# Pauses ahead of two mixer steps, a first norm fed by a spread row, and a norm in one operation, in a fp32 encoder trunk on one core

## The chip, the cores and the metric

The kernel runs on one core of a Trainium2 chip. Its time is device microseconds (us) per execution; the median of three runs before is 1455.33 us (1454.59 to 1459.27).

## The reference

Two layers work on 256 tokens of width 1024, in float32. Each is a half-step feed-forward block, a mixer of three branches (GLA, S5, FoX), a cross attention to 256 memory tokens, and a second feed-forward block. Every block has a norm before and behind it:

```
def rms_norm(x, g):
    y = x * rsqrt(mean(x * x) + EPS)
    return y * g
for l in range(DEPTH):
    x = x + 0.5 * rms_norm(swiglu(rms_norm(x, ffn1_pre_g), w_gu, w_down), ffn1_post_g)
    p = rms_norm(x, mix_pre_g) @ w_in         # GLA's q, k, v, gates; S5's input u; FoX's q, k, v; branch gates
    x = x + rms_norm((sum_b sigmoid(gate_b) * up_b(mixer_b)) @ w_mix_out, mix_post_g)
    x = x + rms_norm(cross_attn(rms_norm(x, xa_pre_g), rms_norm(mem)), xa_post_g)
    x = x + 0.5 * rms_norm(swiglu(rms_norm(x, ffn2_pre_g), w_gu, w_down), ffn2_post_g)
```

In GLA, `g = cumsum(log_a)` sets decays: keys are multiplied by `exp(g_last - g)` for the chunk states, and by `exp(-g)` and `exp(g)` for the products inside a chunk. S5 is a complex scan whose output `y` goes through a gelu and a 256x256 gate product.

## The kernel before

Every matrix is kept as a high and a low part (`wh`, `wl`, `xth`, `xtl`: `split`, L234), and each product is three TensorE passes (`mm3`, L248). Weights stream from HBM in pieces of 128x1024 (512 KB): SyncE issues the transfer into one of five `wf` buffers, ScalarE casts it to `wh`, VectorE subtracts for `wl`; seven `wh`/`wl` pairs form a ring, so about five pieces stand ready ahead of TensorE. One half of a `proj_cols` takes one piece and 24 products of 256 columns.

Each engine runs its instructions in the order in which the program text gives them. Side work (GLA, S5, FoX, the S5 set-up) is written as generators; `run_tasks` is called after each half of a projection (a tick) and advances each by one step; `yield n` puts off the next step by n ticks. `finish` runs a generator to its end at once, whatever pauses are left. So a `yield` sets where a step's instructions stand in every engine's queue, and not a time.

GLA (`gla`, L798): `gla_gates` forms z, g and the three exponentials; then VectorE multiplies keys (L815 to L817: `dg` is the key with its decay), TensorE transposes `dg` (L821), ScalarE copies it out (L823); VectorE then forms `qb` (L827, L829), which the products at L840 read; the o products are L866 and L869; the last transposes are L889. S5 (`s5`, L896): L910 and L922 are its first products, the scan is L926, L945 the output products, L954 the gelu's last step; then `yd` is written to DRAM (L958), read back in another layout as `yv` (L961), and `yv` is the operand of L967. In the FoX projections L1003 copies TensorE's result out, and L1007 writes rows of `fq` that a transfer of a one-hot table (L993) fills first.

A block's end is `boundary` (L446). Token tile 0's last products are done first, and its norm runs on ScalarE, VectorE and GpSimd beside tile 1's products: `post2` (L412) updates x, `pre1` squares x on ScalarE (L381), multiplies x by the gain on VectorE (L419, L422), adds the sums (L387), GpSimd raises to -1/2 (L388), and `scale` (L427) multiplies by that factor; TensorE then transposes (L433).

The start (`run`, `first`): twelve warm products of zeros; transfers of tile 0 of x, of the gain (one row spread to 128 partitions by the transfer, 512 KB), of the identity, of two weight pieces, of tile 1, of more weights. `first` norms tile 0, transposes it and multiplies it by the first four pieces (`go(0)`, L336) while tile 1 is normed; then transposes tile 1 and runs `go(1)`. Two of the first `wl` are made by GpSimd.

Of the kernel before, what the change touches and what calls it, by code (L numbers as in the profile page):

```python
# [8 lines left out]
F32 = mybir.dt.float32  # L9
# [4 lines left out]
ALU = mybir.AluOpType  # L14
# [6 lines left out]
EPS = 1e-6  # L21
# [9 lines left out]
WB = 7  # L31
WF = 5
HALF = 1024
WARM = 12
TAIL = 5

C_ID, C_FM, C_P2, C_HM, C_END = 0, 128, 512, 520, 524
# [17 lines left out]
class Trunk:  # L55
# [23 lines left out]
    def make_plan(self, depth):  # L79
        a = self.a  # L80
        self.plan, self.parts = [], []

        def add(ap, n=2048):
            for c in range(0, n, HALF):
                self.plan.append(ap[:, c:min(c + HALF, n)])

        def ffn(l, i):
            gu, dn = a[f"ffn{i}_gu"], a[f"ffn{i}_dn"]
            q = 0
            for j in range(NFT):  # L90
                add(gu[l, j])
                if j >= 4 and j % 2 == 0:
                    n = min(q + 2, NFT - TAIL)
                    for k in range(q, n):
                        add(dn[l, k], D)
                    q = n
            for k in range(q, NFT):
                add(dn[l, k], D)
            self.parts.append(len(self.plan))

        for l in range(depth):
            ffn(l, 1)
            for q in range(2):
                add(a["w_gvr"][l, q])
            add(a["w_small"][l], 512)
            for q in (0, 1, 2, 4):
                add(a["w_cols"][l, q])
            for q in range(2):
                add(a["w_fv"][l, q])

            def gate(b, c):
                add(a["w_cols"][l, 6 + 4 * b + c])

            def up(b, c):
                if b == 2:
                    add(a["w_fup"][l, c], 1024)
                else:
                    add(a["w_up"][l, b, c], 512)

            for c in (0, 1):  # L120
                gate(0, c)
            for q in (3, 5):
                add(a["w_cols"][l, q])
            for b, c in ((0, 0), (0, 2), (2, 0), (2, 2)):
                if (b, c) != (0, 0):
                    gate(b, c)
# [16 lines left out]
        self.pool_every = 0  # L143


    def house(self, homes):
# [13 lines left out]
            self.raw[self.n_dma] = (wf, n)  # L160
            self.n_dma += 1

    def split_next(self, eng=None):
# [12 lines left out]
        if eng is None and self.pool_every and i % self.pool_every == 0:  # L176
            eng = self.nc.gpsimd
        self.split(h[:, 0:n], lo[:, 0:n], wf[:, 0:n], eng)
        self.ready[i] = (h, lo)
        self.n_split += 1  # L180
        self.fetch(i + 1 + WF)

    def ahead(self, lag=1):
        while self.room(lag):
# [46 lines left out]
            self.ahead()  # L231


    def split(self, h, lo, src, eng=None, vector=False):  # L234
# [5 lines left out]
        (eng or self.nc.vector).tensor_tensor(full(lo), src, h.bitcast(F32), op=ALU.subtract)  # L240

    def split_ps(self, h, lo, ps):
        h, src = full(h), full(ps)
# [168 lines left out]
            self.nc.vector.scalar_tensor_tensor(xx, o, r, xx, op0=ALU.mult, op1=ALU.add)  # L412

    def pre1(self, src, g):
        V = self.nc.vector
        hn = self.work()
        o, i, gg = halves(hn), halves(src), halves(g)
        ss = [self.sumsq(i[0], 0)]
        V.tensor_tensor(o[0], i[0], gg[0], op=ALU.mult)  # L419
        ss.append(self.sumsq(i[1], 1))  # L420
        r = self.rstd(ss, EPS)
        V.tensor_tensor(o[1], i[1], gg[1], op=ALU.mult)  # L422
        return hn, r

    def scale(self, hn, r):
        for h in halves(hn):
            self.nc.vector.tensor_scalar(h, h, r, None, op0=ALU.mult)  # L427

    def turn(self, hn, q):
        ps = self.bank()  # L430
# [15 lines left out]
    def boundary(self, banks, tail, half, width=None, fill=None):  # L446
        nc = self.nc
        go_tail, last = tail
        gpost, gpre = self.gp, self.gn
        self.ahead(0)  # L450
        go_tail(0)
        square, times, second = self.post1(banks[0], gpost, half)
        square(0)
        times(0)
        y0 = second()
        xt = self.xt()
        st = {}

        def turn(t, q):
            self.pre3(t, q, self.turn(st[t], q), xt)  # L460

        def early():
            self.post2(0, *y0)
            h0, r0 = self.pre1(self.x[:, 0], gpre)
            st["p1"] = self.post1(banks[1], gpost, half)
            st["p1"][0](0)
            self.scale(h0, r0)
            st["p1"][1](0)
            st[0] = h0
            turn(0, 0)  # L470

        self.free(last)
        go_tail(1, (2 * last - 1, early))
        p = self.turn(st[0], 1)
        y1 = st["p1"][2]()
        self.pre3(0, 1, p, xt)

        def late():
            self.post2(1, *y1)
            h1, r1 = self.pre1(self.x[:, 1], gpre)  # L480
            self.scale(h1, r1)
            st[1] = h1
# [12 lines left out]
        self.free(4)  # L495
        self.ahead()
        return xt, ps

    def store(self, banks, tail):
        nc, out = self.nc, self.a["out"]  # L500
        for t in range(2):
# [5 lines left out]
            for n, (o, xx) in enumerate(zip(halves(y), halves(self.x[:, t]))):  # L507
                nc.vector.scalar_tensor_tensor(xx, o, r, xx, op0=ALU.mult, op1=ALU.add)
                nc.sync.dma_start(out[t * 128:(t + 1) * 128, n * 512:(n + 1) * 512], xx)

    def first(self, g, width):
        V = self.nc.vector
        xt = self.xt()

        def norm(t):
            hn = self.work()
            r = self.rstd([self.sumsq(x, n) for n, x in enumerate(halves(self.x[:, t]))], EPS)
            for o, x, gg in zip(halves(hn), halves(self.x[:, t]), halves(g)):
                V.scalar_tensor_tensor(o, x, r, gg, op0=ALU.mult, op1=ALU.mult)
            return hn  # L520

        h = norm(0)
        p0 = self.turn(h, 0)
        p1 = self.turn(h, 1)
        self.split_next(self.nc.gpsimd)
        self.pre3(0, 0, p0, xt, True)
        self.pre3(0, 1, p1, xt)
        self.split_next()
        h = norm(1)
        self.split_next(self.nc.gpsimd)  # L530
        out, go = self.head(width)
        go(0, xt)
        self.turned(1, h, xt)
        go(1, xt)
        self.free(4)
        self.ahead()
        return xt, out
# [263 lines left out]
    def gla(self, l, psm, vg, sgg, com, pool):  # L801
# [14 lines left out]
        V.tensor_tensor(kie, ks, ieg, op=ALU.mult)  # L816
        V.tensor_tensor(keg, ks, eg, op=ALU.mult)  # L817
        S.copy(ae, eg[:, 63:255:64])
        pkt = self.pbank(1)
        for t in range(2):  # L820
            T.transpose(pkt[:, t * 128:(t + 1) * 128], kd[:, t * 128:(t + 1) * 128], ident)  # L821
# [75 lines left out]
    def s5(self, l, com):  # L897
# [5 lines left out]
        def tt(o, x, y, op):  # L903
            V.tensor_tensor(o, x, y, op=op)

        yield 3
        vr, vi = self.bank(), self.bank()
        for i, v in enumerate((vr, vi)):
            for j in range(8):
# [419 lines left out]
    def run(self, depth=L):  # L1329
# [4 lines left out]
        nc.vector.memset(zero, 0.0)  # L1334
        zero = zero.rearrange("p a b -> p (a b)").bitcast(BF16)
        warm = self.bank()
        for i in range(WARM):
# [179 lines left out]
```

## Time and profile before

| | |
|---|---|
| median of 3 runs | 1455.33 us |
| the profiled execution | 1458.61 us, span 1456.8 us, mean granted TensorE clock 0.990 |
| TensorE products busy | 1425.2 us (98%) |
| VectorE, ScalarE, GpSimd busy | 936.4 us (64%), 715.2 us (49%), 68.8 us (5%) |
| transfers | 257.52 MB, 177 GB/s on average |

TensorE's share counts a product that runs at half clock as busy too, so what it loses stands in two places: idle time ahead of an instruction (with what ended it), and stretches in which the granted clock (PEclk) is 0.50, that is 1.2 instead of 2.4 GHz.

### The profile page before, as it was taken

What the parts mean: (1) busy time and instruction counts of PE and PEld (TensorE: products, weight loads), DVE (VectorE), ACT (ScalarE), POOL (GpSimd) and SP (SyncE); (2) the same over time, 40 slices, a digit from 0 to 9 for tenths busy, and PEclk for the clock granted to TensorE, in tenths of its full rate; (3) what the DMA queues carried; (4) which work ended last, traced back from release to release, by engine and by line L of the source; (5) the groups of instructions that cost most, each with busy time, mean ns of one, the idle gap of its engine ahead of it and who ended that gap; (6) DMA issues with size and microseconds to landing.
All of it is one profiled execution on the core that took longest, in us unless ns stands there. A gap on an engine that the chain in (4) does not pass through costs nothing.

```text
span 1456.8 us, 24663 instructions
## 1 busy us (share of the span) xinstructions
PE 1425.2 (98%) x9972; PEld 1314.7 (90%) x9972; DVE 936.4 (64%) x1408; ACT 715.2 (49%) x1129; POOL 68.8 (5%) x60
## 2 busy tenths in 40 slices
PE   8999998999999999999999999989999999999998
PEld 7999988889979989999999999888899898899997
DVE  6787566766587667555577775666556866665553
ACT  5444446355455545444454455454544655454442
POOL 1000000000210000000001000000012100000000
PEclk9999999999999999999999999999999999999999
DMA  7664637245566436655646556362565474375551
GB/s 282 217 195 144 214 121 215 93 130 180 201 213 212 149 131 206 210 186 181 203 147 215 175 194 191 126 191 91 159 222 162 162 237 160 103 248 184 188 189 44
DMA packets 76034, 257.52 MB, mean 177 GB/s; under 512 B 8688, under 2 KB 11792, under 8 KB 75920
## 3 DMA queue, kind: packets, MB, share of 16 engines
q1 hardware_dynamic: 75920, 255.95, 54.0%
q8 instruction: 78, 1.28, 0.3%
q14 instruction: 36, 0.29, 0.1%
HBM read 253.82 MB, written 2.10 MB: 176 GB/s over the span
## 4 chain that ended last, share of the span: by engine, by line
PE 86%; DVE 5%; ACT 4%; issue 2%; DMA 2%; POOL 1%; SPq 0%; DVEq 0%; POOLq 0%; ACTq 0%
PE mm L250 57%; PE pa L250 21%; PE mm L336 3%; ACT wh L239 1%; DVE wl L240 1%; PE mm L433 1%; DMA wf<-in_xa_k 1%; ACT junk L381 1%; DVE acc L1213 1%; POOL rr L388 1%; PE mm L1053 1%; PE mm L727 1%; PE pa L945 0%; PE mm L910 0%; DVE xtl L1210 0%
## 5 line engine op out<-in xcount | busy, mean ns | idle before, releaser
L240 DVE TENSOR_TENSOR wl<-wf,wh 128x1024 fp32r<-128x1024 f32 (+1 forms) x436 | 520.2, 1206 | 264.6 <-ACT wh L239 263.6
L250 PE MATMUL mm<-xth,wh 128*128 128x256 f32 (+1 forms) x2000 | 570.1, 285 | 0.0
L250 PE MATMUL mm<-xth,wl 128*128 128x256 f32 (+1 forms) x2000 | 567.5, 284 | 0.0
L250 PE MATMUL mm<-xtl,wh 128*128 128x256 f32 (+1 forms) x2000 | 566.7, 283 | 0.0
L239 ACT CAST wh<-wf 128x1024 fp32r<-128x1024 f32 (+1 forms) x442 | 446.0, 1029 | 154.3 <-PE mm L250 63.4
L250 PEld LDWEIGHTS mm<-xth,wh 128*128 128x128 f32 (+1 forms) x2000 | 379.0, 190 | 4.0 <-issue 2.1
L250 PEld LDWEIGHTS mm<-xtl,wh 128*128 128x128 f32 (+1 forms) x2000 | 377.2, 189 | 1.8
L250 PEld LDWEIGHTS mm<-xth,wl 128*128 128x128 f32 (+1 forms) x2000 | 377.9, 189 | 0.0
L250 PE MATMUL pa<-wh,hl 128*128 128x512 f32 x320 | 125.3, 392 | 0.0
L250 PE MATMUL pa<-wl,hh 128*128 128x512 f32 x320 | 125.2, 391 | 0.0
L250 PE MATMUL pa<-wh,hh 128*128 128x512 f32 x320 | 124.8, 390 | 0.0
L558 ACT ACTIVATE sil<-mm 128x256 f32<-128x256 f32 (+1 forms) x96 | 35.1, 366 | 118.0 <-PE mm L250 109.8
L239 ACT CAST hh<-h 128x256 fp32r<-128x256 f32 x80 | 32.5, 406 | 100.5 <-DVE h L560 100.5
L560 DVE TENSOR_TENSOR h<-sil,mm 128x256 f32<-128x256 f32 (+1 forms) x96 | 38.0, 396 | 60.7 <-ACT sil L558 60.7
L388 POOL TENSOR_TENSOR rr<-rv,mhalf 128x1 f32<-128x1 f32 x36 | 27.9, 775 | 954.8 <-DVE rv L387 954.8
L250 PEld LDWEIGHTS pa<-wh,hl 128*128 128x128 f32 x320 | 60.0, 188 | 12.7
L250 PEld LDWEIGHTS pa<-wl,hh 128*128 128x128 f32 x320 | 60.1, 188 | 11.9
L250 PEld LDWEIGHTS pa<-wh,hh 128*128 128x128 f32 x320 | 60.2, 188 | 11.6
L240 DVE TENSOR_TENSOR hl<-h,hh 128x256 fp32r<-128x256 f32 x80 | 34.0, 425 | 37.8 <-ACT hh L239 37.8
L239 ACT CAST xth<-mm 128x512 fp32r<-128x512 f32 x39 | 22.6, 587 | 54.7 <-PE mm L433 23.6
L250 PE MATMUL mm<-mt,wh 128*128 128x256 f32 x256 | 47.6, 288 | 0.0
L240 DVE TENSOR_TENSOR xtl<-mm,xth 128x512 fp32r<-128x512 f32 x40 | 27.2, 688 | 27.8 <-ACT xth L239 27.8
(286 smaller groups left out, 1773.4 us busy)
## 6 DMA issues: line engine op xcount, KB each, us to landing
wf<-in_ffn_gu SPq DMA_DIRECT2D x176, 512.0 KB, 4.5
wf<-in_ffn_dn SPq DMA_DIRECT2D x88, 512.0 KB, 4.5
wf<-in_w_cols SPq DMA_DIRECT2D x72, 512.0 KB, 4.1
wf<-in_w_mix SPq DMA_DIRECT2D x16, 512.0 KB, 4.4
wf<-in_xa_k SPq DMA_DIRECT2D x16, 512.0 KB, 4.4
wf<-in_xa_q SPq DMA_DIRECT2D x16, 512.0 KB, 4.4
wf<-in_xa_v SPq DMA_DIRECT2D x16, 512.0 KB, 4.5
wf<-in_xa_o SPq DMA_DIRECT2D x16, 512.0 KB, 4.8
```

The lines of the kernel that those rows point to most:

```text
L239: self.nc.scalar.copy(h, src)
L240: (eng or self.nc.vector).tensor_tensor(full(lo), src, h.bitcast(F32), op=ALU.subtract)
L250: self.nc.tensor.matmul(out, lhsT=lhs[i], rhs=rhs[j], start=start and n == 0, stop=stop and n == 2)
L336: self.nc.tensor.matmul(out, lhsT=xt[b][:, kk, tk], rhs=w[2 * g + i][a][:, k * width:(k + 1) * width], start=first, stop=last)
L381: self.nc.scalar.activation(jk, src, AF.Square, scale=math.sqrt(f / D), accum_out=s)
L388: self.nc.gpsimd.tensor_tensor(r, v, self.mhalf[:, 0:1], op=ALU.pow)
L433: self.nc.tensor.transpose(ps[:, i * 128:(i + 1) * 128], hn[:, k * 128:(k + 1) * 128], self.ident)
L558: nc.scalar.activation(sil, gate, AF.Silu)
L560: nc.vector.tensor_tensor(h, sil, up, op=ALU.mult)
L727: T.matmul(ps[0:32, j * 128:(j + 1) * 128], lhsT=cz[:, i, 4 * q + j], rhs=wa[:, i, 4 * q + j].rearrange("p k h -> p (k h)"), start=i == 0, ...
L1053: T.matmul(o[:, 0:256], lhsT=fv[:, 0, c], rhs=p[:, 0:256], start=True, stop=False)
L1213: V.tensor_tensor(acc[:, c], acc[:, c], gt, op=ALU.add)
```

## The change

Five edits. (1) GLA yields two ticks ahead of its first transposes, so these and everything behind them in GLA stand two ticks later. (2) S5's first pause is 6 ticks and not 3, and the one behind the `yv` transfers 5 and not 3. (3) The norm ahead of a block multiplies x by factor and gain in one operation behind the factor (`pre2`), where it was a product with the gain ahead of the factor and one with the factor behind it. (4) At the start the gain comes as one row of 4 KB, ahead of x, and TensorE spreads it to 128 partitions by two products with a row of ones, between six warm products; VectorE squares the second half of tile 0. (5) `first` makes all four first `wl` on VectorE, in another order, and puts tile 1's first transposes into `go(0)` and tile 1's second half of the norm behind them.

```
-WARM = 12
+WARM = 6
...
     def pre1(self, src, g):
-        ss = [self.sumsq(i[0], 0)]
-        V.tensor_tensor(o[0], i[0], gg[0], op=ALU.mult)
-        ss.append(self.sumsq(i[1], 1))
-        r = self.rstd(ss, EPS)
-        V.tensor_tensor(o[1], i[1], gg[1], op=ALU.mult)
-        return hn, r
-
-    def scale(self, hn, r):
-        for h in halves(hn):
-            self.nc.vector.tensor_scalar(h, h, r, None, op0=ALU.mult)
+        i, gg = halves(src), halves(g)
+        r = self.rstd([self.sumsq(x, n) for n, x in enumerate(i)], EPS)
+        return i, gg, r
+
+    def pre2(self, x, g, r):
+        hn = self.work()
+        for o, i, gg in zip(halves(hn), x, g):
+            self.nc.vector.scalar_tensor_tensor(o, i, r, gg, op0=ALU.mult, op1=ALU.mult)
+        return hn
...
+        def factor(t):
+            x = halves(self.x[:, t])
+            ss = [self.sumsq(x[0], 0)]
+            if t == 0:
...
+                V.scalar_tensor_tensor(jk, x[1], 1.0 / D, x[1], op0=ALU.mult, op1=ALU.mult, accum_out=ss[1])
+            else:
+                ss.append(self.sumsq(x[1], 1))
+            r[t] = self.rstd(ss, EPS)
+        def times(t, n):
+            V.scalar_tensor_tensor(halves(hn[t])[n], halves(self.x[:, t])[n], r[t], g[n], op0=ALU.mult, op1=ALU.mult)
+        factor(0)
+        times(0, 0)
+        times(0, 1)
+        p = [self.turn(hn[0], q) for q in range(2)]
+        low = self.split_next(defer=True)
+        self.pre3(0, 0, p[0], xt, True)
+        self.pre3(0, 1, p[1], xt)
+        low()
         self.split_next()
+        factor(1)
+        self.split_next()
+        times(1, 0)
+        self.split_next()
         out, go = self.head(width)
+        def early():
+            self.pre3(1, 0, self.turn(hn[1], 0), xt)
+            times(1, 1)
+        go(0, xt, (40, early))
+        self.pre3(1, 1, self.turn(hn[1], 1), xt)
         go(1, xt)
...
         S.copy(ae, eg[:, 63:255:64])
+        yield 2
         pkt = self.pbank(1)
...
-        yield 3
+        yield 6
         vr, vi = self.bank(), self.bank()
...
-        yield 3
+        yield 5
         pg = self.pbank(2)
...
+        nc.sync.dma_start(row, a["ffn1_pre_g"][0:1])
+        gn = [self.pbank(2), self.pbank(3)]
         for i in range(WARM):
             nc.tensor.matmul(warm, lhsT=zero[:, 0:128], rhs=zero, start=i == 0, stop=i == WARM - 1)
+            if i == 3:
+                for p, rr in zip(gn, halves(row)):
+                    nc.tensor.matmul(p, lhsT=ones, rhs=rr, start=True, stop=True)
...
-        gn = self.gain(a["ffn1_pre_g"][0])
```

VectorE in the first layer's GLA, from the decayed keys on (`dg`, `g` and `zz` are the three products with the keys, `wl` a weight's low part, `qb` the operand of the in-chunk products). Before:

```order
L815 TENSOR_TENSOR dg<-ks,dg 128x256
L816 TENSOR_TENSOR g<-ks,ieg 128x256
L817 TENSOR_TENSOR zz<-ks,eg 128x256
L240 TENSOR_TENSOR wl<-wf,wh 128x1024
L1007 TENSOR_SCALAR fq<-fc 8x1024
L827 TENSOR_TENSOR eg<-qs,eg 128x256
L829 TENSOR_TENSOR qb<-eg,cst 128x1024
L240 TENSOR_TENSOR wl<-wf,wh 128x1024
L827 TENSOR_TENSOR ieg<-qs,ieg 128x256
L829 TENSOR_TENSOR qb<-ieg,cst 128x1024
```

and in the changed kernel:

```order
L832 TENSOR_TENSOR dg<-ks,dg 128x256
L833 TENSOR_TENSOR g<-ks,ieg 128x256
L834 TENSOR_TENSOR zz<-ks,eg 128x256
L241 TENSOR_TENSOR wl<-wf,wh 128x1024
L1025 TENSOR_SCALAR fq<-fc 8x1024
L241 TENSOR_TENSOR wl<-wf,wh 128x1024 x2
L1023 COPY fk<-fc 8x1024
L845 TENSOR_TENSOR eg<-qs,eg 128x256
L847 TENSOR_TENSOR qb<-eg,cst 128x1024
L241 TENSOR_TENSOR wl<-wf,wh 128x1024
L845 TENSOR_TENSOR ieg<-qs,ieg 128x256
L847 TENSOR_TENSOR qb<-ieg,cst 128x1024
```

The decayed keys stand where they stood; two more weight pieces and the copy into `fk` stand ahead of the first `qb`.

SyncE's queue in the first layer's mixer, around S5's transfers `yd` and `yv`. Before:

```order
L159 DMA wf<-in_w_up 128x512 x2
L159 DMA wf<-in_w_cols 128x1024 x3
L958 DMA yd<-z_2862 128x512
L961 DMA yv<-yd 128x1x128 x4
L159 DMA wf<-in_w_cols 128x1024
L159 DMA wf<-in_w_up 128x512
L993 DMA fq<-in_onehot 64x1024
L994 DMA fk<-in_onehot 64x1024
L159 DMA wf<-in_w_up 128x512
```

and in the changed kernel:

```order
L158 DMA wf<-in_w_cols 128x1024 x3
L158 DMA wf<-in_w_up 128x512
L1011 DMA fq<-in_onehot 64x1024
L1012 DMA fk<-in_onehot 64x1024
L158 DMA wf<-in_w_up 128x512
L976 DMA yd<-z_2935 128x512
L979 DMA yv<-yd 128x1x128 x4
```

S5's two transfers stand behind the one-hot tables and three weight pieces that they stood ahead of.

VectorE at a block's end, in the norm of tile 0 (`x` is updated, `rv` the mean square, `nw` the normed tile). Before:

```order
L412 SCALAR_TENSOR_TENSOR x<-nw,rr,x 128x512 x2
L419 TENSOR_TENSOR nw<-x,gain 128x512
L387 TENSOR_SCALAR rv<-ss 128x1
L422 TENSOR_TENSOR nw<-x,gain 128x512
L427 TENSOR_SCALAR nw<-nw,rr 128x512 x2
```

and in the changed kernel:

```order
L405 TENSOR_TENSOR nw<-pa,gain 128x512
L417 SCALAR_TENSOR_TENSOR x<-nw,rr,x 128x512 x2
L392 TENSOR_SCALAR rv<-ss 128x1
L427 SCALAR_TENSOR_TENSOR nw<-x,rr,gain 128x512 x2
L405 TENSOR_TENSOR nw<-pa,gain 128x512
```

Nothing stands beside GpSimd's power any more, and two operations of another kind stand behind it.

## Rows read from the trace of the kernel before

**Rows 1.** The waits of TensorE over the whole execution (us in total, times, longest), and one of VectorE's:

```profile
PE pa L821 <- DVE dg L815: 9.9, 2, 5.0
PE mm L433 <- DVE nw L427: 6.0, 7, 2.5
PE mm L336 <- ACT wh L239: 1.8, 1, 1.8
PE pa L967 <- DMA yv<-yd: 1.7, 1, 1.7
...
PE pa L967 <- issue: 0.7, 1, 0.7
...
DVE fq L1007 <- DMA fq<-in_onehot: 12.8, 2, 6.9
```

**Rows 2.** Busy time by stretch (us; then PE, PEld, DVE, ACT, POOL with instructions, PEclk, DMA share, GB/s): the start, both GLA waits and what lies about them:

```profile
0.00:20.00 20.00, 14.94 (x69) 10.83 (x70) 10.87 (x14) 8.63 (x14) 6.05 (x8) 0.83 0.82 301
9.20:16.00 6.80, 5.58 (x25) 5.52 (x26) 4.45 (x5) 5.90 (x9) 4.27 (x3) 0.50 1.02 401
236.00:241.00 5.00, 5.00 (x44) 4.89 (x42) 4.23 (x6) 4.52 (x7) 0.00 (x0) 1.00 0.65 183
241.00:246.00 5.00, 0.10 (x1) 0.00 (x0) 3.54 (x7) 1.88 (x5) 0.00 (x0) 0.87 0.62 197
246.00:251.40 5.40, 5.35 (x25) 5.35 (x26) 3.85 (x6) 1.32 (x2) 0.00 (x0) 0.50 0.29 79
965.60:968.30 2.70, 2.69 (x13) 2.69 (x14) 1.24 (x3) 1.32 (x2) 0.00 (x0) 0.50 0.19 58
```

**Rows 3.** The timeline of VectorE in the first layer's GLA (start us, us, instruction, count, idle time before it and what ended it):

```profile
245.57 0.42 DVE L815 TENSOR_TENSOR dg<-ks,dg 128x256 f32<-128x256 f32 x1
...
246.25 0.42 DVE L817 TENSOR_TENSOR zz<-ks,eg 128x256 f32<-128x256 f32 x1
248.12 1.23 DVE L240 TENSOR_TENSOR wl<-wf,wh 128x1024 fp32r<-128x1024 f32 x1 [1.46 <-ACT wh L239]
249.38 0.69 DVE L1007 TENSOR_SCALAR fq<-fc 8x1024 f32<-8x1024 f32 x1
250.09 0.43 DVE L827 TENSOR_TENSOR eg<-qs,eg 128x256 f32<-128x256 f32 x1
250.56 1.22 DVE L829 TENSOR_TENSOR qb<-eg,cst 128x1024 f32<-128x1024 f32 x1
...
255.57 1.23 DVE L829 TENSOR_TENSOR qb<-ieg,cst 128x1024 f32<-128x1024 f32 x1
...
260.76 0.68 DVE L1005 COPY fk<-fc 8x1024 f32<-8x1024 f32 x1
```

**Rows 4.** The timeline of ScalarE there, same columns:

```profile
246.77 0.37 ACT L823 COPY zl<-pa 128x256 f32<-128x256 f32 x1 [2.27 <-PE pa L821]
...
251.81 1.20 ACT L1003 ACTIVATE fq<-mm 64x512 f32<-64x512 f32 x2 [3.72 <-PE mm L250]
```

**Rows 5.** The timelines of TensorE, GpSimd and VectorE at the end of GLA, first layer, same columns:

```profile
281.36 0.68 PE L869 MATMUL pa<-vg,zz 64*64 64x64 f32 x8
...
283.68 1.65 POOL L880 TENSOR_TENSOR orr<-ov,mhalf 128x8 f32<-128x8 f32 x1 [68.45 <-DVE ov L879]
...
287.05 0.69 DVE L884 SCALAR_TENSOR_TENSOR zz<-zl,sgg 128x512 f32<-128x512 f32 x1
```

**Rows 6.** The timeline of SyncE's queue at S5's transfers, first layer, same columns:

```profile
301.20 0.33 SPq L958 DMA_DIRECT2D yd<-z  x1
303.27 2.34 SPq L961 DMA_DIRECT2D yv<-yd  x4
...
306.69 0.52 SPq L993 DMA_DIRECT2D fq<-in_onehot  x1
```

**Rows 7.** The timeline at the end of the first layer's mixer, same columns:

```profile
433.18 0.68 DVE L422 TENSOR_TENSOR nw<-x,gain 128x512 f32<-128x512 f32 x1
433.41 0.86 POOL L388 TENSOR_TENSOR rr<-rv,mhalf 128x1 f32<-128x1 f32 x1 [2.75 <-DVE rv L387]
...
434.31 0.88 DVE L427 TENSOR_SCALAR nw<-nw,rr 128x512 f32<-128x512 f32 x2 [0.44 <-POOL rr L388]
...
434.94 0.63 PE L433 MATMUL mm<-cst,nw 128*128 128x128 f32 x4 [1.96 <-DVE nw L427]
...
437.68 0.55 POOL L388 TENSOR_TENSOR rr<-rv,mhalf 128x1 f32<-128x1 f32 x1 [3.41 <-DVE rv L387]
```

**Rows 8.** The timeline of the start, same columns:

```profile
1.64 0.43 SPq L254 DMA_DIRECT2D gain<-in_ffn_pre_g  x1
...
6.55 1.41 DVE L519 SCALAR_TENSOR_TENSOR nw<-x,rr,gain 128x512 f32<-128x512 f32 x2 [0.67 <-POOL rr L388]
...
7.36 1.31 PE L433 MATMUL mm<-cst,nw 128*128 128x128 f32 x8 [1.16 <-DVE nw L519]
...
9.33 1.04 ACT L239 CAST wh<-wf 128x1024 fp32r<-128x1024 f32 x1 [3.70 <-DMA wf<-in_ffn_gu]
...
14.71 3.52 DVE L519 SCALAR_TENSOR_TENSOR nw<-x,rr,gain 128x512 f32<-128x512 f32 x2 [0.67 <-POOL rr L388]
...
19.42 0.74 PE L336 MATMUL mm<-wl,xth 128*128 128x256 f32 x4 [0.96 <-DVE wl L240]
...
21.27 0.73 PE L336 MATMUL mm<-wh,xth 128*128 128x256 f32 x4 [0.24 <-ACT xth L239]
```

More of the change, by code (lines that the diff above doesn't have):

```diff
@@ L142, in make_plan @@
         self.raw, self.ready, self.homes = {}, {}, {}
-        self.pool_every = 0
     def house(self, homes):
@@ L161, in fetch, with split_next @@
             self.n_dma += 1
-    def split_next(self, eng=None):
+    def split_next(self, eng=None, defer=False):
         i = self.n_split
@@ L175, in split_next @@
             lo = self.wp.tile([128, HALF], F32R, tag="wl", name="wl")
-        if eng is None and self.pool_every and i % self.pool_every == 0:
-            eng = self.nc.gpsimd
-        self.split(h[:, 0:n], lo[:, 0:n], wf[:, 0:n], eng)
+        low = self.split(h[:, 0:n], lo[:, 0:n], wf[:, 0:n], eng, defer=defer)
         self.ready[i] = (h, lo)
@@ L181, in split_next @@
         self.fetch(i + 1 + WF)
+        return low
     def ahead(self, lag=1):
@@ L231, in rest, with split @@
             self.ahead()
-    def split(self, h, lo, src, eng=None, vector=False):
+    def split(self, h, lo, src, eng=None, vector=False, defer=False):
         h = full(h)
@@ L239, in split, with low @@
             self.nc.scalar.copy(h, src)
-        (eng or self.nc.vector).tensor_tensor(full(lo), src, h.bitcast(F32), op=ALU.subtract)
+        def low():
+            (eng or self.nc.vector).tensor_tensor(full(lo), src, h.bitcast(F32), op=ALU.subtract)
+        if defer:
+            return low
+        low()
     def split_ps(self, h, lo, ps):
@@ L414, in pre1 @@
     def pre1(self, src, g):
-        V = self.nc.vector
+        i, gg = halves(src), halves(g)
+        r = self.rstd([self.sumsq(x, n) for n, x in enumerate(i)], EPS)
+        return i, gg, r
+    def pre2(self, x, g, r):
         hn = self.work()
-        o, i, gg = halves(hn), halves(src), halves(g)
-        ss = [self.sumsq(i[0], 0)]
-        V.tensor_tensor(o[0], i[0], gg[0], op=ALU.mult)
-        ss.append(self.sumsq(i[1], 1))
-        r = self.rstd(ss, EPS)
-        V.tensor_tensor(o[1], i[1], gg[1], op=ALU.mult)
-        return hn, r
-    def scale(self, hn, r):
-        for h in halves(hn):
-            self.nc.vector.tensor_scalar(h, h, r, None, op0=ALU.mult)
+        for o, i, gg in zip(halves(hn), x, g):
+            self.nc.vector.scalar_tensor_tensor(o, i, r, gg, op0=ALU.mult, op1=ALU.mult)
+        return hn
     def turn(self, hn, q):
@@ L463, in early @@
             self.post2(0, *y0)
-            h0, r0 = self.pre1(self.x[:, 0], gpre)
+            h0 = self.pre1(self.x[:, 0], gpre)
             st["p1"] = self.post1(banks[1], gpost, half)
             st["p1"][0](0)
-            self.scale(h0, r0)
+            st[0] = self.pre2(*h0)
             st["p1"][1](0)
-            st[0] = h0
             turn(0, 0)
@@ L479, in late @@
             self.post2(1, *y1)
-            h1, r1 = self.pre1(self.x[:, 1], gpre)
-            self.scale(h1, r1)
-            st[1] = h1
+            st[1] = self.pre2(*self.pre1(self.x[:, 1], gpre))
         if fill is not None:
@@ L513, in first @@
         xt = self.xt()
[L515 to L527, printed above, removed]
+        hn = [self.work() for _ in range(2)]
+        r = [None, None]
+        def factor(t):
+            x = halves(self.x[:, t])
+            ss = [self.sumsq(x[0], 0)]
+            if t == 0:
+                ss.append(self.per.tile([128, 1], F32, tag="ss1", name="ss", bufs=4))
+                jk = halves(hn[1])[1]
+                V.scalar_tensor_tensor(jk, x[1], 1.0 / D, x[1], op0=ALU.mult, op1=ALU.mult, accum_out=ss[1])
[11 more added lines that the diff above has]
+        self.pre3(0, 1, p[1], xt)
+        low()
         self.split_next()
-        h = norm(1)
-        self.split_next(self.nc.gpsimd)
+        factor(1)
+        self.split_next()
+        times(1, 0)
+        self.split_next()
         out, go = self.head(width)
-        go(0, xt)
-        self.turned(1, h, xt)
+        def early():
[3 more added lines that the diff above has]
+        self.pre3(1, 1, self.turn(hn[1], 1), xt)
         go(1, xt)
@@ L1336, in run @@
         warm = self.bank()
+        ones = self.ei[0:1, 0:2].rearrange("p a b -> p (a b)")
+        nc.vector.memset(ones, 1.0)
+        row = self.per.tile([128, D], F32, tag="gain", name="gain", bufs=2)[0:1]
+        nc.sync.dma_start(row, a["ffn1_pre_g"][0:1])
+        gn = [self.pbank(2), self.pbank(3)]
         for i in range(WARM):
             nc.tensor.matmul(warm, lhsT=zero[:, 0:128], rhs=zero, start=i == 0, stop=i == WARM - 1)
+            if i == 3:
+                for p, rr in zip(gn, halves(row)):
+                    nc.tensor.matmul(p, lhsT=ones, rhs=rr, start=True, stop=True)
         for xx, src in zip(halves(self.x[:, 0]), halves(a["x"][:, 0])):
             nc.sync.dma_start(xx, src)
-        gn = self.gain(a["ffn1_pre_g"][0])
         nc.sync.dma_start(self.ident, a["cst"][:, C_ID:C_ID + 128])
```

## The prediction

> **What bounds the kernel now.** I read the page first: TensorE is 98% busy, so only what it waits and what it does at half clock can be won. Then the list of its waits [rows 1]: in it the reader is to see that two waits ahead of GLA's first transposes (9.9 us) are the largest, followed by seven ahead of a block's transposes behind the norm (6.0), those at the start (1.8 here, 1.16 and 0.96 in its timeline [rows 8]) and two ahead of S5's gate product (1.7 and 0.7). Then the table of stretches [rows 2]: before the first GLA wait 44 products took 5.0 us, 0.114 each; in the 5.0 us of the wait almost nothing ran; and behind it 25 took 5.35 at a granted clock of 0.50, the lower level of 1.2 GHz, 0.214 each. The clock fell after TensorE had stood still, and the price of the wait is therefore more than its length. In the second layer 13 products in 2.69 us were slow, 0.207 each. The timelines of single engines come last, for who is late and by how much.
>
> **GLA's pause.** The keys with decay are written at 245.57 + 0.42 = 245.99 [rows 3], and TensorE had got there at 241.1. Nothing in VectorE's queue up to that row moves, and what stands there waits for ScalarE and not for TensorE's later products. The transposes now stand 48 products later, at 241.1 + 48 x 0.114 = 246.6, which is 0.6 us behind the keys: no wait, and no reason for the clock to fall. What goes is 9.9 us of waiting and the slow stretches, 25 x (0.214 - 0.114) = 2.5 and 13 x (0.207 - 0.114) = 1.2: 13.6 in both layers.
>
> What is late next? The products with `qb`, since VectorE now makes three weight pieces and the copy into `fk` ahead of it. From 246.67: three pieces at 1.23, 0.69 for `fq`, 0.68 for `fk`, 0.43 and 1.22 for the first `qb`, then 1.23, 0.43 and 1.23 for the second [rows 3] is 256.3 if nothing overlaps; neighbours there overlap by about 0.1 each (two of 0.42 start 0.68 apart from 245.57 on), so 255.4 to 256.3. ScalarE's casts for these pieces now follow the copies of `fq` and of the keys (1.20 and 0.37 [rows 4]), whose products end 2.8 us after 241.1; I count them done in time. TensorE arrives after transposes (0.35), 24 products of 256 columns (2.7) and 24 of 512 (twice the columns, 5.5): 255.2, and needs the second `qb` 0.25 later. The wait is between 0 and 0.9 per layer; I take 0.5, so 1.0 comes back.
>
> At its end GLA has fewer pauses than it asks for, as it is finished at once behind the two gate projections. Its last operand was written at 287.05 + 0.69 = 287.74, 5.7 us behind the end of the last o products (281.36 + 0.68), with GpSimd's power (1.65) the longest piece [rows 5]. TensorE now has 48 products (5.5), some small ones of FoX and, newly, S5's sixteen output products between the two (at 0.114 each or more, 1.8 or more): 7.3 or more against 5.7, and what S5's and FoX's operations in VectorE's queue add to that. I count 1 to 4 us to spare, and no wait.
>
> **S5's pauses.** The 2.4 us of waiting for `yv` [rows 1] go: `yd` and `yv` are issued later (301.20 and 303.27 before [rows 6]), but their reader stands about 12 half-projections behind S5's output products, some 25 us, against about 16 before. The one-hot tables go out ahead of `yd` now, so VectorE's wait for them (12.8 us in both layers [rows 1], behind which TensorE did not wait, since five weight pieces stood ready) may shorten; that gives nothing. Ends: 2.4 won, or nothing if `yv` is late by the same again. I take 2.4.
>
> **The norm in one operation.** Ahead of the factor two products with the gain fall away, beside ScalarE's squares, worth nothing by themselves; but one of them ran while GpSimd raised to a power: 0.86 us beside it, against 0.55 beside an operation that read PSUM [rows 7]. So I let the factor come 0.31 earlier. Behind it the first half takes longer: from its start to TensorE's transposes 434.94 - 434.31 = 0.63 with the old operation [rows 7], 7.36 - 6.55 = 0.81 with one of the new form [rows 8]. The sum is 0.31 - 0.18 = 0.13 won per waiting transpose, seven times: 0.9. The second half ends 0.2 later than now and is hidden by products. Ends: 0.9 won, and 1.8 lost if GpSimd is not faster (below).
>
> The Trainium skill, "VectorE: DVE Perf Modes", section on the perf-mode tier table, says that a float32 operation with a scalar runs at two elements a cycle from SBUF and one with two tensors at one. The halves in the trace agree (0.44 against 0.70), and by that rule alone this edit would cost and not give.
>
> **The start.** The row is issued first, and takes the slot of 0.43 us that the gain's transfer takes now [rows 8], so x comes 0.43 later; with VectorE squaring the second half I put the first transposes at about 7.9 instead of 7.36. The first weight piece waits behind 512 KB less: at 301 GB/s [rows 2] that is 1.7 us, so it lands at 7.6 and not 9.33 [rows 8]. Its cast (1.04) is then no longer what ends last; TensorE's first product follows the transposes at about 9.4, where it now starts at 10.4. VectorE makes all four `wl`, but its pair of norm operations no longer takes 3.52 us beside GpSimd in place of 1.41 [rows 8]. A new wait comes: between tile 1's first and second transposes stand a copy by ScalarE (0.6), a subtraction (0.7) and the second norm half (0.7), with 8 products (0.9) beside them, so TensorE stands some 1.5 us where it now stands 0.96. `go(1)` started at 21.27. I get 19.1 if the clock is back early, 20.3 if it is as slow as now from 9.2 to 16.0 [rows 2], and after a new slow stretch behind the wait (price as above, up to 2.5) the equal of 22.8. I take 20.0: 1.3 won, with ends 2.2 won and 1.5 lost. Six warm products fewer cost nothing, since the row's products and x's wait fill the time.
>
> **The sum.** 13.6 - 1.0 + 2.4 + 0.9 + 1.3 = 17.2 us. On the profiled execution's own 1458.61 that is 1441.4; this execution lies 3.3 us above the median of the runs, 1455.33, on which the forecast is made: 1438.
>
> **Rivals.**
> Rival A, the wait moves to `qb`: VectorE is the engine that is late in GLA, and pauses only move the place. If it can use none of the gaps that it has now, the second `qb`, at 256.8 now, comes two pieces and a copy later, 3.1 us, at 259.9; TensorE would wait 4.5 there, with a slow stretch of about 1.8 behind it, in both layers: 12.6 given back less the 1.0 counted, 1449.6. For it: the second `qb` already ends late [rows 3]. Against it: VectorE's gaps there of 1.46 and more waited for ScalarE, and ScalarE for TensorE, which no longer stands.
> Rival B, the start gives nothing: the wait of 1.5 between tile 1's transposes pulls the clock down once more. 1438 + 2.8 = 1441. For it: the clock was down there already.
> Rival D, the norm costs: GpSimd's 0.86 has another reason, so the factor comes no earlier and 0.26 more of VectorE's operation stands behind it seven times: 1.8 lost in place of 0.9 won, 1441. That is what the Trainium skill's rule above would give alone.
> Rival C, slower than before: GLA's end has no pause left. If VectorE, with S5's products, FoX's row maxima and the weight pieces in one queue, is later by more than the 1 to 4 us to spare, TensorE waits at the last transposes, and the clock falls again (1.9 a layer). From 6.7 us of waiting a layer on all that was won is gone; at 9 us it is 2 x (9 + 1.9) on top of 1438, 1460. Against it: each of these operations is under 1.3 us.
>
> **How the numbers follow.** The forecast has 0.56, B 0.18, A 0.14, D 0.10, C 0.02. The low end takes the start's best end, no wait at `qb` and some of the two long norm waits (1.96 [rows 7] and 2.5 [rows 1]) with it: 1433. The high end takes B and D together, and A where it comes half: 1446; whole A and C are left out. What a measurement of this kernel can tell from no change is 0.3%, 4.4 us: faster means below 1451. All but C and the worst of A lie there: 0.94 faster, 0.04 within, 0.02 slower.
>
> **What would show it.** Right: no wait ahead of GLA's first transposes and of S5's gate product in TensorE's list; no granted clock of 0.50 behind them; the power on GpSimd at 0.55 in every norm at a block's end; first product at about 9.4 us, `go(1)` at about 20. Wrong: a wait ahead of the products with `qb` above 1 us (A), a slow stretch at about 20 to 23 us (B), waits behind the norm grown (D), or a wait ahead of GLA's last transposes (C). A gain under 10 us would say that GLA's 13.6 did not come.

## The result and the profile after

The changed kernel takes 1439.53 us (median of 4 runs, 1437.95 to 1440.16) where the kernel before takes 1454.96 in the same measurement: a ratio of 0.9886, interval 0.9865 to 0.9907. Measured once more beside the last experiments it took 1437.76 against 1455.91, 0.9876 [0.9861, 0.9891]. The forecast was 1438. The profiled execution takes 1437.95, with a span of 1436.1.

The page of the changed kernel, busy time of the engines:

```profile
PE 1419.9 (99%) x9970; PEld 1308.1 (91%) x9970; DVE 927.3 (65%) x1385; ACT 712.9 (50%) x1127; POOL 60.4 (4%) x58
```

Between the two profiled executions the span falls by 20.7. TensorE's busy time is 5.3 of it (1425.2 to 1419.9: fewer products at half clock, less 1.1 that it is busier up to `go(1)`), and 15.4 is its idle time (1456.8 - 1425.2 = 31.6 before, 1436.1 - 1419.9 = 16.2 after). This pair shows more than the medians, since the kernel before was profiled in a longer execution than its median (1458.61) and the changed one in its shortest.

TensorE's waits in the changed kernel (us in total, times, longest; the whole list, which answers to [rows 1]):

```profile
PE mm L434 <- DVE nw L427: 5.1, 5, 2.2
PE mm L434 <- DVE nw L528: 1.5, 2, 1.2
PE pa L255 <- ACT xth L1232: 1.2, 2, 0.6
PE mm L1361 <- DVE er L1352: 1.2, 1, 1.2
PE pa L1040 <- DVE nm L1044: 0.4, 2, 0.2
```

The transposes of GLA (9.9) and S5's gate product (1.7 and 0.7) are gone from the list. The waits behind the norm (L434 here, L433 before) are 5.1 where they were 6.0.

Busy time by stretch, same columns as in [rows 2]:

```profile
0.00:20.00 20.00, 17.29 (x75) 11.73 (x76) 11.58 (x20) 8.40 (x13) 1.32 (x6) 1.00 0.84 287
240.00:245.00 5.00, 5.00 (x46) 5.00 (x44) 3.53 (x9) 3.72 (x7) 0.00 (x0) 1.00 0.50 166
245.00:250.00 5.00, 5.00 (x36) 4.61 (x35) 4.88 (x6) 3.91 (x6) 0.00 (x0) 1.00 0.63 168
250.00:255.00 5.00, 4.87 (x23) 3.30 (x22) 4.93 (x6) 1.30 (x2) 0.00 (x0) 1.00 1.00 360
```

Where 5 us stood nearly empty before, TensorE is busy all but 0.13 us and at full clock; VectorE has the load, 4.88 and 4.93 of 5 us. Its timeline there, with TensorE's first transposes and the products with the second `qb` (start us, us, instruction, count):

```profile
243.79 0.42 DVE L832 TENSOR_TENSOR dg<-ks,dg 128x256 f32<-128x256 f32 x1
...
253.07 1.22 DVE L847 TENSOR_TENSOR qb<-ieg,cst 128x1024 f32<-128x1024 f32 x1
```

```profile
244.83 0.38 PE L839 MATMUL pa<-cst,dg 128*128 128x128 f32 x2
253.58 0.65 PE L858 MATMUL pa<-qb,g 128*64 128x256 f32 x2
254.35 0.43 PE L858 MATMUL pa<-qb,zz 128*64 128x256 f32 x1
```

The keys are written 0.62 us ahead of the transposes. The second `qb` ends at 254.29 and its product starts at 254.35, after a gap of about 0.1: TensorE and VectorE come to this point nearly together.

### The profile page after: what moved, and what is told of

The parts are those of the page before. It is cut to its first block, busy times and chain, and to the rows that moved or that the text cites. A ratio compares the mean times of both kernels' runs of the same rounds, so it can differ in the third digit from the quotient of the medians.

```text
span 1436.1 us, 24637 instructions
## 1 busy us (share of the span) xinstructions
PE 1419.9 (99%) x9970; PEld 1308.1 (91%) x9970; DVE 927.3 (65%) x1385; ACT 712.9 (50%) x1127; POOL 60.4 (4%) x58
## 4 chain that ended last, share of the span: by engine, by line
PE 87%; DVE 6%; ACT 3%; issue 2%; DMA 2%; POOL 0%; SPq 0%; DVEq 0%; POOLq 0%; ACTq 0%
PE mm L255 56%; PE pa L255 21%; PE mm L341 4%; DVE wl L241 1%; ACT wh L237 1%; PE mm L434 1%; DMA wf<-in_xa_k 1%; ACT junk L386 1%; DVE acc L1231 1%; PE mm L1071 1%; PE mm L744 1%; PE mm L928 1%; PE pa L963 0%; DVE xtl L1228 0%; PE pa L1059 0%
## 5 line engine op out<-in xcount | busy, mean ns | idle before, releaser
L393 POOL TENSOR_TENSOR rr<-rv,mhalf 128x1 f32<-128x1 f32 x36 | 23.5, 653 | 960.0 <-DVE rv L392 960.0
L1186 ACT ACTIVATE gt<-mm 128x512 f32<-128x512 f32 x24 | 14.3, 598 | 61.6 <-PE mm L255 55.1
```

The lines of the kernel that those rows point to most:

```text
L393: self.nc.gpsimd.tensor_tensor(r, v, self.mhalf[:, 0:1], op=ALU.pow)
```

## The experiments

The first four runs take the edits one by one on the kernel before, which took 1457.66 us (median of 31 runs) beside them.

**GLA's pause alone.**

```
         S.copy(ae, eg[:, 63:255:64])
+        yield 2
```

> The kernel before with GLA's pause of two ticks alone. Theory (the forecast's own term): both waits of 4.9 and 5.0 us ahead of GLA's first transposes go, no granted clock of 0.50 near 245 and 965 us, about 0.5 us a layer of waiting at the products with qb instead: 12.6 us less than before, some 1442.5. The waits ahead of the gate product (2.4), behind the norm (6.0) and the start (second go at 21.3 us) stay as they are. Rival 1: the clock's stretches differ from one execution to the next, so only the waits count surely: 9.9 - 1.0 = 8.9 less, 1446. Rival 2: the gain of the whole change, 15.4, comes from GLA's pause alone and the other edits give nothing: 1439.5.

Measured: 1458.03 us, ratio 1.0006 [0.9994, 1.0017]. Nothing, where 12.6 was expected; neither rival had this. In its list of waits and its timeline of TensorE:

```profile
PE mm L911 <- DMA u<-ud: 6.3, 2, 3.3
```

```profile
247.01 0.38 PE L822 MATMUL pa<-cst,dg 128*128 128x128 f32 x2
250.45 5.15 PE L911 MATMUL mm<-u,m 128*128 128x64 f32 x32 [3.07 <-DMA u<-ud]
```

The 9.9 us at GLA's transposes are gone, and 6.3 us stand ahead of S5's first products instead, whose 32 small products then take 5.15 us. The clock fell again; busy time by stretch, PEclk third from the end:

```profile
247.00:250.45 3.45, 0.39 (x4) 0.18 (x3) 3.10 (x4) 2.18 (x3) 0.00 (x0) 1.00 0.44 98
250.45:256.00 5.55, 5.55 (x35) 5.55 (x36) 1.05 (x2) 0.00 (x0) 0.00 (x0) 0.69 0.92 317
```

The chain of this kernel (start us, us, what) says what S5 waited for: its operand `u` goes to DRAM and comes back in another layout, as `yv` does later.

```profile
242.62 4.25 DMA ud<-su
...
248.21 2.04 DMA u<-ud
250.25 0.20 issue
250.45 5.15 PE mm L911 x32
255.60 4.64 PE mm L250 x24
```

That this wait takes all of the gain can be added up. In both layers 9.9 us of waiting and 3.7 of slow products go, 13.6. Back come 6.3 of waiting and, in each layer, some 3.4 of slow products: the 32 products with `u` and the 24 behind them take 9.8 in the first layer, where the kernel before needs 3.5 + 2.9, and 9.9 in the second. That is 13.1.

The kernel before has the same trip, and no wait there. Its SyncE queue and TensorE:

```profile
246.78 2.77 SPq L1083 DMA_DIRECT2D u<-ud  x4
```

```profile
254.45 3.68 PE L910 MATMUL mm<-u,m 128*128 128x64 f32 x32
```

Four issues end at 249.55, and the last of them starts at 249.11. The 2.04 above run from the start of the last issue (in that run the four issues end at 248.64, and `u` is there at 250.25). So in the kernel before `u` is there at about 251.15, 3.3 us ahead of its product. GLA's wait and the slow products behind it had pushed that product back by 4.9 + 2.5 = 7.4 us. Whoever takes these 7.4 away runs into `u`, by some 4 us on this count; the measured waits are 3.07 and 3.27.

**S5's pauses alone.**

```
-        yield 3        (ahead of S5's first products)
+        yield 6
-        yield 3        (behind the yv transfers)
+        yield 5
```

> The kernel before with S5's longer pauses alone. Theory: the waits of 1.7 and 0.7 us ahead of S5's gate product go and nothing else changes: 2.4 less, 1452.5. Rival: the one-hot tables and the weight pieces that now go out ahead of S5's transfers, or S5's products in other places, shift the wait elsewhere (GLA's waits grow from 9.9 by as much), and the time stays at 1455.

Measured: 1453.18 us, 0.9970 [0.9961, 0.9980], 4.5 us less. The waits at the gate product are gone from the list and GLA's 9.9 is unchanged, so the rival is out. That is about 2 us more than the wait. The mean granted clock is 0.9932 over its ten runs against 0.9919 over the 31 of the kernel before, which on 1457 us is 1.9 us; the rest is the 2.4 of the waits. Why fewer stretches are slow was not separated: the two at half clock behind the mixers' last norms, which the profile of the kernel before has (below), are missing in this run's profile, and in that of GLA's pause alone as well, so they may come and go between executions.

**The norm alone** (`pre1`, `pre2` and `boundary` as in the change).

> The kernel before with the norm in one operation behind the factor alone. Theory: GpSimd's power takes 0.55 in place of 0.86 us, 0.18 more stands behind it, TensorE's waits behind the norm fall from 6.0 to about 5.1 in all: 0.9 less, 1454. Rival: the power stays at 0.86 or the rest of the chain takes up what it gives: waits of 6.0 or more, 1455 to 1457.

Measured: 1457.47 us, 1.0002 [0.9990, 1.0014], which holds both 0.9 less and nothing. The trace tells more. The end of the first mixer and the list of waits:

```profile
431.39 0.55 POOL L388 TENSOR_TENSOR rr<-rv,mhalf 128x1 f32<-128x1 f32 x1 [2.75 <-DVE rv L387]
431.97 1.41 DVE L422 SCALAR_TENSOR_TENSOR nw<-x,rr,gain 128x512 f32<-128x512 f32 x2 [0.73 <-POOL rr L388]
...
432.87 0.63 PE L429 MATMUL mm<-cst,nw 128*128 128x128 f32 x4 [1.71 <-DVE nw L422]
```

```profile
PE mm L429 <- DVE nw L422: 4.7, 5, 2.0
```

The power takes 0.55 where it took 0.86 [rows 7], from the operation's start to TensorE it is 0.90 where it was 0.63, and the waits fall by 1.3. How little of these 1.3 is the norm's stands below.

**The start alone** (row, six warm products, order of `first`).

> The kernel before with the edits at the start alone (row spread by TensorE, six warm products, all first wl on VectorE, tile 1's transposes in two parts). Theory: second go at 19.8 to 20.0 us where it was 21.3, so 1.3 to 1.5 less, 1453.6. Rival: the wait of 1.2 between tile 1's transposes, or the later first transposes, pulls the granted clock down for longer than before: 1455 or more. If all four runs of this set add up to the whole change they give 12.6 + 2.4 + 0.9 + 1.3 = 17.2 by the forecast's terms; the whole change measured 15.4.

Measured: 1456.31 us, 0.9990 [0.9975, 1.0005]; its second `go` starts at 19.80 where it was 21.27 [rows 8]. The 1.4 are in line with the theory, and the interval holds nothing as well.

The four gave -0.4 + 4.5 + 0.2 + 1.4 = 5.7 us, where the whole change gives 15.4. The next runs, beside 1457.45 (median of 13) for the kernel before, look for the other ten.

**GLA's pause with S5's first pause.**

```
+        yield 2        (GLA)
-        yield 3        (ahead of S5's first products)
+        yield 6
```

> The kernel before with GLA's pause and S5's longer first pause (6 ticks), the second pause behind yv left at 3. Theory after the first four runs: GLA's pause alone gave nothing because the wait moved to S5's first products, whose operand u comes back from DRAM at 250.25 us; three ticks more put these behind it. So the waits at GLA's transposes and at u both vanish with their slow products: 10 to 13 us less than before, 1445 to 1448 beside 1457.7; a wait ahead of the gate product (yv) of 1 to 2.4 us stays. Rival: S5's first pause only moves the wait once more, to the products behind it (z, w, the scan), and the time stays above 1454.

Measured: 1441.38 us, 0.9897 [0.9879, 0.9914], 16.1 less, where 10 to 13 were expected. Both waits are gone, and the one at the gate product too, which was to stay: its pause was still 3. GLA's pause, which gave nothing alone, gives this with one line changed in another task.

**With both of S5's pauses** (the second at 5 as well).

> GLA's pause and both of S5's longer pauses, norm and start as before. Theory: all the waits of the mixer are gone; what is missing to the whole change is the start (1.3) and the norm (0.9): 1442 to 1443. Rival: norm and start are worth more together with the mixer's edits than the 1.4 and 0.4 that they gave alone, and this run stands at 1445 or more.

Measured: 1439.76 us, 0.9884 [0.9869, 0.9899]: 17.7 less, more than either side expected. The mixer's three `yield`s are all but 0 to 2 us of the change (1439.53, and 1437.76 when measured again).

**S5's second pause alone.**

> The kernel before with the pause behind yv at 5 ticks alone, S5's first pause left at 3. Theory: this half of the S5 edit is what takes the wait at the gate product away: 2.4 less in waits, and up to 2 more where products behind that wait ran at half clock, 1453 to 1455; the waits of 9.9 at GLA's transposes stay. Rival: the longer first pause gave the 4.5 us of the S5 run, by moving S5's 48 small products to another place; then this run stands at 1457.

Measured: 1452.19 us, 0.9971 [0.9959, 0.9983]. The S5 run with both had 0.9970. So its 4.5 are the second pause's; the first, by the difference of the two, gives nothing without GLA's, and GLA's nothing without the first. The first pause quite alone, and GLA's with the second but without the first, were not run.

**One more operation beside the power,** in the changed kernel:

```
+        self.nc.vector.tensor_tensor(halves(hn)[1], i[1], gg[1], op=ALU.mult)
```

> The changed kernel with one more product of x and the gain on VectorE between the mean square and the multiplication by factor and gain (its result is overwritten, so nothing of the output changes): it stands beside GpSimd's power, as in the kernel before. Theory: the power takes 0.86 again and not 0.55 in the norms at a block's end, TensorE's waits behind the norm rise from 5.1 by 7 x 0.31 = 2.2 us, 1441.5. Rival: the power was slower for another reason, it stays at 0.55 and the 0.68 of VectorE decides by itself (0.13 a norm, 0.9 in all): 1440.4.

Measured: 1442.10 us (1441.98 to 1442.19), 0.9902 [0.9884, 0.9920]. The end of its first mixer, and its list:

```profile
423.06 0.68 DVE L423 TENSOR_TENSOR nw<-x,gain 128x512 f32<-128x512 f32 x1
```

```profile
423.29 0.87 POOL L393 TENSOR_TENSOR rr<-rv,mhalf 128x1 f32<-128x1 f32 x1 [2.75 <-DVE rv L392]
```

```profile
PE mm L435 <- DVE nw L428: 7.6, 7, 2.6
```

The power is back at 0.87 and the waits rise from 5.1 to 7.6, for 2.2 forecast: each of the five short ones grows by 0.28 to 0.37 or comes back into the list. The two expected times lie 1.1 apart, too near for the times to choose; the trace does. VectorE's product over two operands in SBUF is what slows GpSimd here; the norm's one operation removes it.

Such an operation beside the power is not enough, though. At the start of the changed kernel a split over two SBUF operands stands beside the power for 0.46 us, as long as the product does above, and the power takes 0.56:

```profile
13.83 0.56 POOL L393 TENSOR_TENSOR rr<-rv,mhalf 128x1 f32<-128x1 f32 x1 [6.62 <-DVE rv L392]
13.93 1.23 DVE L241 TENSOR_TENSOR wl<-wf,wh 128x1024 fp32r<-128x1024 f32 x1 [0.17 <-ACT wh L237]
```

That split starts 0.10 behind the power. The product above starts 0.23 ahead of it, and the power ends 0.42 behind the product's end (0.41 in [rows 7]). In one norm of this run the power starts only 0.12 before the product's end, and takes 0.56. So it looks as if the power waits for an operation that is already under way when it starts; that is read off these rows and was not tested by a run.

The last four runs stand beside 1455.91 (median of 7) for the kernel before.

**The changed kernel again.**

> The changed kernel once more, unedited, beside the runs below. Open: the mixer's edits alone stand at 1439.8, and the changed kernel, which has the norm and the start besides, at 1439.5 in four runs, where the forecast gives these two 2.2 us. Theory 1: both are real in every execution (in the profiled ones the start's last product ends 1.7 to 2.0 us earlier), and four runs misjudge it: about 1437.8. Theory 2: in most executions one stretch at half clock (1.7 us) stands behind a mixer's last norm, which the profiled execution happens not to have, and takes the start's gain back: 1439.5, with single runs at 1437.9 and 1439.6 or more.

Measured: 1437.76 us (1437.55 to 1438.75). This is theory 1. The first four runs have a median 1.8 higher, in line with a mean clock of 0.998 in three of them, where three of these four have 0.999. Where their slow stretch lay is not shown, as both profiles were taken of executions without it.

**Without the start** (the mixer's pauses and the norm).

> The changed kernel without the edits at the start (GLA's pause, both S5 pauses and the norm in one operation). Theory 1: the norm gives its 0.9 beside the mixer's edits: 1438.9, and the start the rest. Theory 2: the norm's 0.9 shows in the waits (about 4.7 to 5.0 behind the norm in place of 5.4) but not the start's gain: 1438.9 as well, with the changed kernel no faster than this one. Rival: the norm costs (operations of the new form behind the factor): 1440.5.

Measured: 1439.25 us, 0.9888 [0.9871, 0.9904]; waits behind the norm 5.0. The start is therefore worth 1.5 beside the run above. The norm, from 1439.76 to 1439.25 across two measurements, is worth 0.5 by the times, nothing by the ratios beside each one's kernel before (0.9884 and 0.9888), and 0.4 by the waits (5.4 to 5.0). Neither the start's 1.5 nor this is clear of the noise.

**Tile 0's transposes behind products that need no norm.** At the mixer's end, in the changed kernel:

```
+            self.post2(1, *y1)
+            h1 = self.pre1(self.x[:, 1], gpre)
+            fill(0)
+            self.turned(0, st[0], xt)
+            st[1] = self.pre2(*h1)
+            fill(1)
+            self.turned(1, st[1], xt)
```

> The changed kernel with tile 0's transposes at the mixer's end put behind the first 48 products with the memory, which need nothing of the norm, and tile 1's behind the next 48. Theory: the two longest waits that are left (2.2 and 1.9 us behind the norm at 424.6 and 1133.7) go, and with them any stretch at half clock behind them: 4 us less than the changed kernel, 1435.5, and up to 1.7 more where theory 2 of the unedited run holds, 1433.8. Rival: VectorE, which now turns x and copies the products out later, is late for the cross attention's first projections, and the wait of 2 us a layer only moves: 1439.

Measured: 1436.87 us (1436.68 to 1436.94), 0.9868 [0.9853, 0.9883]: 0.9 less than the changed kernel, not 4. The rival is right in kind. VectorE and TensorE behind the first mixer:

```profile
429.31 4.63 DVE L241 TENSOR_TENSOR wl<-wf,wh 128x1024 fp32r<-128x1024 f32 x4 [0.72 <-ACT wh L237]
433.86 0.69 DVE L241 TENSOR_TENSOR kT<-mm,kT 128x512 fp32r<-128x512 f32 x1
434.46 1.28 DVE L241 TENSOR_TENSOR xtl<-mm,xth 128x512 fp32r<-128x512 f32 x2
435.65 1.41 DVE L427 SCALAR_TENSOR_TENSOR nw<-x,rr,gain 128x512 f32<-128x512 f32 x2
```

```profile
436.54 1.29 PE L434 MATMUL mm<-cst,nw 128*128 128x128 f32 x8 [1.39 <-DVE nw L427]
```

Tile 0's wait of 2.2 is gone. Tile 1's multiplication now stands behind four weight pieces and three operations of other splits, and TensorE waits 1.39 (1.55 in the second layer) at tile 1's transposes.

**And the second half of the first norm ahead of a split.**

```
         def early():
+            times(1, 1)
             self.pre3(1, 0, self.turn(hn[1], 0), xt)
-            times(1, 1)
```

> The same, and at the start VectorE's second half of tile 1's norm ahead of the split of the first half, so that tile 1's second transposes wait 1.2 us less. Theory: 1.2 less than the run before, second go at 18.6 us and not 19.8: about 1434. Rival: the split of the first half, now later by 0.7, holds up the second go, or the clock takes it back: no difference to the run before.

Measured: 1435.96 us (1434.89 to 1438.27), 0.9864 [0.9850, 0.9879]. Its second `go` starts at 18.46, 1.1 us before that of the run above (19.53), and the median is 0.9 lower. Its list has a wait of 0.6 at the products with `qb`: VectorE is now the later of the two there, at the place that rival A named. Its four runs reach over a wider range than those of the run above, so the two can't be ranked. Both medians lie below those of the two kernels of this document, by 0.9 and 1.8 us under the changed one; that is less than the 0.3% that this measurement can tell.

## Why the prediction was right

Time and range held. Of the reasons one was incomplete, in a way that would have failed on GLA's pause alone, and the norm's term was too large.

**GLA's pause.** The forecast read 13.6 us of waits and slow products, and 0.5 a layer of new wait at `qb`. The geometry was right: it put the transposes 0.6 behind the keys (0.62). The keys are written 1.8 earlier than forecast, most of it from the shorter start, and TensorE and VectorE come to `qb` 1 to 2 us earlier, together, at the low end of the forecast's 0 to 0.9. What it missed is the step "what is late next": it followed VectorE's queue to `qb` and to GLA's end, and not the next operand that comes by a transfer. With GLA's edit alone the next late thing is S5's `u`, and the gain is nothing. The sum came out because the change also moves S5's products back. The forecast listed that edit among S5's pauses, and priced these by `yv` alone: that the 13.6 came was luck, as the forecast did not know on what they hung.

**S5's pauses.** On the kernel before, the 2.4 is right for the waits, and is the second pause's alone. In the whole change it is not shown: with GLA's pause and the first one the wait was gone before the second was made longer, and the 1.6 us that this then gave (1441.38 to 1439.76) come with a higher mean clock (0.9952 and 0.9978 over four runs each) and with more idle time of TensorE in the profile, not less (19.0 and 20.4). The first pause, for which the forecast named no effect of its own, decides some 16 us: the two runs with GLA's pause that differ in it alone stand at 1.0006 and 0.9897. In the changed kernel `u` has room, in SyncE's queue and TensorE's:

```profile
244.70 1.77 SPq L1101 DMA_DIRECT2D u<-ud  x4
```

```profile
255.36 3.79 PE L928 MATMUL mm<-u,m 128*128 128x64 f32 x32
```

The four issues end at 246.47 and the last starts at 246.03; the transfer has landed at 248.04 and is used at 255.36: 7.3 us to spare, where the kernel before had 3.3.

**The norm.** The step on GpSimd is right: 0.55 in every norm at a block's end. The size of 0.9 is not. Behind the factor the new form costs 0.90 - 0.63 = 0.27, where the sum took 0.18 (rival D had priced the same step at 0.26). So 0.31 - 0.27 = 0.04 is left per norm, and the rows agree: from the mean square to TensorE's transposes it is 434.94 - 433.05 = 1.89 before and 424.56 - 422.71 = 1.85 after.

```profile
433.05 0.21 DVE L387 TENSOR_SCALAR rv<-ss 128x1 f32<-128x1 f32 x1 [0.34 <-ACT junk L381]
```

```profile
422.71 0.21 DVE L392 TENSOR_SCALAR rv<-ss 128x1 f32<-128x1 f32 x1 [0.94 <-ACT junk L386]
...
424.56 0.63 PE L434 MATMUL mm<-cst,nw 128*128 128x128 f32 x4 [2.22 <-DVE nw L427]
```

The short waits show it too: 0.45, 0.29 and 0.44 before are 0.37, 0.26 and 0.40 after, and the two of 0.17 are too short for the list now. Seven times 0.05 is about 0.3. The rest of the fall from 6.0 to 5.1 lies in the two long waits at the mixers' ends, and these are 1.8 to 2.6 us in the profiles with the old norm and 1.7 to 2.3 in those with the new one (the runs that edit the norm or the mixer's end further left out). That the list shows 0.9 is luck. The Trainium skill's rule that a float32 operation with two tensors from SBUF runs slower than one with a scalar ("VectorE: DVE Perf Modes", perf-mode tier table) agrees with the step behind the factor, 0.90 in place of 0.63; it was not the whole, as the trace's shorter power stood against it.

**The start.** Rows of the changed kernel, same columns as in [rows 8]:

```profile
7.24 1.41 DVE L528 SCALAR_TENSOR_TENSOR nw<-x,rr,pa 128x512 f32<-128x512 f32 x2 [0.67 <-POOL rr L393]
7.59 1.04 ACT L237 CAST wh<-wf 128x1024 fp32r<-128x1024 f32 x1 [2.31 <-DMA wf<-in_ffn_gu]
8.04 1.97 PE L434 MATMUL mm<-cst,nw 128*128 128x128 f32 x8 [0.30 <-DVE nw L528]
10.04 1.19 PE L341 MATMUL mm<-wh,xth 128*128 128x256 f32 x4
...
19.42 0.63 PE L434 MATMUL mm<-cst,nw 128*128 128x128 f32 x4 [1.21 <-DVE nw L528]
19.80 0.72 PE L341 MATMUL mm<-wh,xth 128*128 128x256 f32 x4
```

The weight's cast starts at 7.59, so the weight lands by 7.6 as forecast, the wait between tile 1's transposes is 1.21 for 1.5, and `go(1)` starts at 19.80 for 20.0. The first product comes at 10.04 and not 9.4, for the eight transposes take 1.97 where they took 1.31 [rows 8]. Rival B's fall of the clock behind tile 1's wait did not come.

**Rivals.** A did not come: at `qb` TensorE stands for about 0.1 in the first layer, where the forecast took 0.5, and the list of waits doesn't name it. C did not: GLA's last transposes are in no list. D did not come whole: its cost behind the factor did, and the shorter power outweighs it by 0.04 a norm. On the profiled execution the forecast was 1441.4, and it took 1437.95. The two slow stretches that the kernel before has behind its mixers' last norms, 3.4 and 3.3 us at a clock of 0.50, about 1.7 lost in each, are as much as the 3.5 between; the forecast left them in. The other misses are smaller and go both ways (0.8 less waiting at `qb`, 0.6 less from the norm), and were not added up. In the kernel before and in the changed one:

```profile
435.90:439.30 3.40, 3.40 (x17) 3.20 (x16) 2.58 (x5) 1.76 (x4) 0.55 (x1) 0.50 0.00 0
1152.80:1156.10 3.30, 3.21 (x12) 2.84 (x13) 1.55 (x4) 1.18 (x3) 0.00 (x0) 0.50 0.00 0
```

```profile
424.50:428.00 3.50, 3.44 (x27) 3.29 (x28) 2.87 (x6) 1.65 (x4) 0.55 (x1) 1.00 0.00 0
1133.70:1137.20 3.50, 3.50 (x27) 3.32 (x28) 2.87 (x6) 1.65 (x4) 0.55 (x1) 1.00 0.01 2
```

The waits ahead of them are much the same in both kernels, 1.96 and 2.5 [rows 1, 7] against 2.2 and 1.9, and nothing in the change was made to end these stretches.

**The sum.** By the runs the mixer's three pauses gave 17.7, where the forecast's terms for them make 13.6 - 1.0 + 2.4 = 15.0, and norm and start 0.2 to 2.0 together (within the noise), where it had 2.2. So the total is nearer than its parts.

## What to carry to other kernels

A wait that is taken away was also the cover of what stands behind it. Before its length is booked as a gain, list the next operands that come by a transfer, and read for each how long it lay ready: 3.3 us of slack against 7.4 us taken out would have told that a new wait of some 4 us comes in each layer, with its own slow products. Two edits that look like repairs of two separate waits can be one repair: here GLA's pause gave nothing alone, S5's first pause nothing that the difference of two runs shows, and both together 16 us.

## What was not expected of the hardware

A wait of about 2 us does not by itself decide whether the clock falls. Behind 1.96 and 2.5 it was at 0.50 in the kernel before, behind 2.2 and 1.9 at 1.00 in the changed one, and behind 2.59 in the run with one more operation at 0.66 on average:

```profile
425.00:430.00 5.00, 4.91 (x26) 4.57 (x27) 4.10 (x8) 1.90 (x5) 0.55 (x1) 0.66 0.00 0
```

At the start of the changed kernel the table of stretches gives a clock of 1.00 for the first 20 us, yet four products take 1.05 us at 11.88 and 0.64 at 14.30:

```profile
11.88 1.05 PE L341 MATMUL mm<-wh,xth 128*128 128x256 f32 x4
...
14.30 0.64 PE L341 MATMUL mm<-wh,xtl 128*128 128x256 f32 x4
```

There the pace of the products and the recorded clock differ. So a table without a slow stretch doesn't prove that nothing ran slowly; the time of one product does.
